# Loading the weights of dt on SyncE's queue ahead of the first tile of x, instead of on ScalarE's queue

## The chip, the cores and the metric

The kernel runs on one core of a Trainium2 chip. The metric is the device time of one execution in microseconds, lower is better. The profile of an execution covers a span that is a little shorter than that time: the span starts and ends with what the hardware profiler records on the engines.

Five engines work side by side, each through its own list of instructions in order: TensorE (PE, with PEld for its weight loads), VectorE (DVE), ScalarE (ACT), GpSimd (POOL) and SyncE (SP). Transfers between the chip's memory (HBM) and the on-chip SBUF are issued by an engine's instruction, and then run on 16 DMA engines. In this kernel nearly all loads are issued by SP; two of the first ones are issued by ACT.

## The reference

One layer of a hybrid decoder: 16 meta tokens are put ahead of 512 tokens, all 528 pass a norm, one large projection `w_in`, a pooling branch and a Mamba-2 branch, gates, an output projection and an MLP. What matters here is the start:

```
h = jnp.concatenate([meta, x], axis=1)
u = rmsnorm(h, mix_norm_w[i])
proj = u @ w_in[i]
xbc = proj[..., OFF_XBC:OFF_DT]
dt_raw = proj[..., OFF_DT:OFF_GATE]
...
dt = jax.nn.softplus(dt_raw + dt_bias)
```

`dt_raw` is a projection to only 32 columns, one for each head; `xbc` is one to 4096 columns.

## The kernel before

Features lie on the 128 partitions and tokens along the free axis, so x is eight tiles `xt[k]` of 128x528 (`NK` = 8, `L` = 528). Products run in a float32 form that TensorE takes in one pass with fewer bits, so every operand is split into a high part and a remainder: ACT casts to get the high part (`xh`, `whi`), DVE subtracts to get the rest (`xl`, `wlo`), and each product is three matmuls, high times high (line 141), high times rest (142) and rest times high (144). Line numbers are those of the profile.

**Weights** come as blocks of 128x1024 from `in_w`, in the order in which they are used. `block_tiles` hands out a buffer `raw` (three of them) and the split ones `whi` and `wlo` (four of each); `block_part` loads a block or a part of it on SP's queue (line 69), casts it on ACT (70) and subtracts on DVE (71). Block 0 holds the weights of dt: 256 columns, the 32 heads for each of the eight k. On the chip they are repeated four times (`once`, `spread`), so that the product has 128 rows. Block 1 holds the first block of B, its output tile is `px`.

**The start.** ACT issues `vs` (line 107: all vectors, the norm's scale among them) and then the 256 columns of dt's weights (line 178). SP issues x tile 0 (line 187), a quarter of block 1 (line 69), x tiles 1 and 2, the rest of block 1, x tiles 3 to 7, and then block after block. Meanwhile TensorE runs nine matmuls on a tile of ones (`WARM`, line 183), whose results nobody uses. Then:

- line 195: ACT casts the dt weights of k = 0 and 1; line 196: DVE subtracts
- line 190: ACT scales x tile k by the norm's weight, writes `xh`; line 191: DVE writes `xl`
- lines 200, 201: for k = 0 the products for dt (`pdt`, two runs of tokens) and for B (`px`)
- lines 203, 204: the dt weights of k = 2 to 7; line 206: the rest of block 1
- lines 209 to 225: the same for k = 2 to 7, with the squares of x for the norm (`square`, lines 211 to 215). The norm's factor is put on the results afterwards, so the products need not wait for it.

After the start the same pattern holds to the end: SP loads a block as soon as a `raw` buffer is free, ACT and DVE split it, TensorE multiplies.

**The order.** The text above is not quite the order in which an engine runs things. The framework's scheduler puts each engine's list together at build time, by priority (the order of the text) among what it expects to be ready, and adds the waits on semaphores. `ea` (line 279), for instance, stands far below the start in the text; it needs only `vs`, and it is ACT's first computation in the profile. Each engine then keeps its list strictly, waits included.

```
wdt, wB = block_tiles(), block_tiles()
b, raw, hi, lo = wdt
nc.scalar.dma_start(raw[:, :256], w[b, :, :256])
...
x_load(0)
act.copy(spread(hi)[:, :2], once[:, :2])
...
x_split(0)
block_part(wB, slice(0, 256))
```

Of the kernel before, what the change touches and what calls it, by code (L numbers as in the profile page):

```python
# [46 lines left out]
def kernel(ctx: ExitStack, tc, xT, x, w, vec, fnw, out):  # L47
    nc = tc.nc
# [126 lines left out]

    wdt, wB = block_tiles(), block_tiles()
    b, raw, hi, lo = wdt
    nc.scalar.dma_start(raw[:, :256], w[b, :, :256])
    spread = lambda t: t.rearrange("p (k c h) -> p k c h", c=4, h=HEADS)
    once = raw[:, :256].rearrange("p (k h) -> p k h", h=HEADS).unsqueeze(2).to_broadcast([P, NK, 4, HEADS])  # L180

# [872 lines left out]
```

## Time and profile before

| | |
|---|---|
| median of 3 runs | 1032.47 us (1031.5 to 1032.63) |
| the profiled execution, its own time | 1032.51 us |
| its span | 1030.8 us |
| PE busy | 1021.6 us of the span |
| DVE, ACT busy | 711.9, 541.3 us |
| moved by DMA | 105.62 MB, mean 102 GB/s |

How to read the views that follow: the timeline lists an engine's instructions in order, start, duration, engine, line, operation, what it writes and what it reads; in square brackets stands how long the engine was idle just before, and who released it. `ACTq` and `SPq` are the parts of ACT and SP that issue transfers. The chain of waits is followed back from the last instruction: at each step to what released it, or to the instruction before it on its engine. A transfer's "us to landing" counts from the issue to the moment when its semaphore says that all data is there. "PE" durations in the timeline are of single matmuls, which overlap; the chain shows their spacing.

### The profile page before, as it was taken

How to read it: one execution, taken by the hardware profiler on the slowest of the kernel's cores; microseconds unless marked ns; L12 is line 12 of the kernel's file. 1: busy time of each engine (PE TensorE's matmuls, PEld its weight loads, DVE VectorE, ACT ScalarE, POOL GpSimd, SP SyncE). 2: the span in 40 equal slices, each digit the busy share in tenths (PEclk: the TensorE clock that was granted, in tenths of full speed). 3: DMA queues.
4: the chain of work that ended last, by engine and by line, in shares of the span. 5: the costliest groups of instructions: out<-in, count | busy, mean ns of one | idle time of the engine just before them, and what ended most of it. 6: DMA issues, size and time to landing. Idle time of an engine off the chain costs nothing.

```text
span 1030.8 us, 14032 instructions
## 1 busy us (share of the span) xinstructions
PE 1021.6 (99%) x5721; PEld 883.2 (86%) x5721; DVE 711.9 (69%) x934; ACT 541.3 (53%) x706; POOL 9.9 (1%) x24
## 2 busy tenths in 40 slices
PE   9999999999999999999999999999999999999997
PEld 8889989998879898988998888888888888888886
DVE  7978787687646586878664345646686676776866
ACT  7775868586627339573443123345544355354444
POOL 0100000000000000000000000000000000000000
PEclk9999999999999999999999999999999999999999
DMA  6333051414332321413233323533323323333112
GB/s 232 95 139 102 22 164 31 154 46 139 102 107 79 104 102 41 146 54 114 78 105 99 102 82 102 204 127 132 89 83 122 109 80 120 101 102 123 42 41 82
DMA packets 29280, 105.62 MB, mean 102 GB/s; under 512 B 3296, under 2 KB 4256, under 8 KB 28192
## 3 DMA queue, kind: packets, MB, share of 16 engines
q1 hardware_dynamic: 26352, 92.61, 28.1%
q0 software_dynamic: 2000, 11.08, 2.9%
q8 instruction: 45, 0.74, 0.3%
q10 hardware_dynamic: 864, 1.04, 0.3%
q14 instruction: 19, 0.16, 0.0%
HBM read 102.55 MB, written 2.16 MB: 102 GB/s over the span
## 4 chain that ended last, share of the span: by engine, by line
PE 98%; DVE 1%; DMA 0%; ACT 0%; issue 0%; ACTq 0%
PE px L141 6%; PE px L142 6%; PE px L144 6%; PE pf L88 6%; PE pf L87 6%; PE pf L89 6%; PE alpha L797 3%; PE alpha L798 3%; PE alpha L799 3%; PE pz L141 3%; PE pz L142 3%; PE pz L144 3%; PE py L466 2%; PE pp L142 2%; PE pso L87 2%; PE pp L141 2%
## 5 line engine op out<-in xcount | busy, mean ns | idle before, releaser
L70 ACT CAST whi<-raw 128x1024 fp32r<-128x1024 f32 (+1 forms) x139 | 144.2, 1043 | 266.3 <-PE pf L88 59.9
L71 DVE TENSOR_TENSOR wlo<-raw,whi 128x1024 fp32r<-128x1024 f32 (+1 forms) x139 | 168.7, 1215 | 147.7 <-ACT whi L70 140.4
L141 PE MATMUL px<-uh,whi 128*128 128x264 f32 (+1 forms) x448 | 121.2, 290 | 0.7 <-DVE ct L330 0.7
L142 PE MATMUL px<-ul,whi 128*128 128x264 f32 (+1 forms) x448 | 118.9, 285 | 0.0
L88 PE MATMUL pf<-vl,whi 128*128 128x512 f32 x256 | 99.8, 390 | 0.0
L89 PE MATMUL pf<-vh,wlo 128*128 128x512 f32 x256 | 99.7, 389 | 0.0
L87 PE MATMUL pf<-vh,whi 128*128 128x512 f32 x256 | 99.6, 390 | 0.0
L144 PE MATMUL px<-uh,wlo 128*128 128x264 f32 (+1 forms) x448 | 90.8, 284 | 0.0
L141 PEld LDWEIGHTS px<-uh,whi 128*128 128x128 f32 x448 | 84.6, 189 | 2.8 <-issue 2.6
L142 PEld LDWEIGHTS px<-ul,whi 128*128 128x128 f32 x448 | 84.8, 189 | 0.3
L144 PEld LDWEIGHTS px<-uh,wlo 128*128 128x128 f32 x448 | 69.4, 188 | 0.3 <-issue 0.3
L748 DVE TENSOR_TENSOR slo<-b,shi 128x1024 fp32r<-128x1024 f32 x35 | 42.7, 1221 | 31.6 <-ACT shi L747 31.6
L747 ACT CAST shi<-b 128x1024 fp32r<-128x1024 f32 x35 | 36.7, 1050 | 51.9 <-PE pf L88 36.5
L88 PEld LDWEIGHTS pf<-vl,whi 128*128 128x128 f32 x256 | 48.0, 188 | 10.0 <-DVE vl L706 0.2
L87 PEld LDWEIGHTS pf<-vh,whi 128*128 128x128 f32 x256 | 48.1, 188 | 9.9
L89 PEld LDWEIGHTS pf<-vh,wlo 128*128 128x128 f32 x256 | 48.1, 188 | 9.9
L797 PE MATMUL alpha<-shi,hh 128*128 128x512 f32 x140 | 54.6, 390 | 0.0
L799 PE MATMUL alpha<-shi,hl 128*128 128x512 f32 x140 | 54.5, 389 | 0.0
L798 PE MATMUL alpha<-slo,hh 128*128 128x512 f32 x140 | 54.5, 389 | 0.0
L809 DVE TENSOR_TENSOR ht<-ht,alpha 128x1024 f32<-128x1024 f32 x35 | 42.6, 1217 | 6.1 <-PE alpha L799 6.1
L141 PE MATMUL pz<-uh,whi 128*128 128x512 f32 x112 | 44.0, 393 | 0.0
L142 PE MATMUL pz<-ul,whi 128*128 128x512 f32 x112 | 43.9, 392 | 0.0
(340 smaller groups left out, 2405.4 us busy)
## 6 DMA issues: line engine op xcount, KB each, us to landing
raw<-in_w SPq DMA_DIRECT2D x137, 512.0 KB, 3.6
b<-in_w SPq DMA_DIRECT2D x28, 512.0 KB, 3.6
abc<-acs_d POOLq DMA_DIRECT2D x8, 1024.0 KB, 7.5
xt<-in_xT SPq DMA_DIRECT2D x8, 264.0 KB, 5.2
ht<-in_x POOLq DMA_DIRECT2D x4, 512.0 KB, 4.9
w<-in_w SPq DMA_DIRECT2D x4, 512.0 KB, 3.5
out_dram<-out SPq DMA_DIRECT2D x4, 320.0 KB, 2.4
out_dram<-out ACTq DMA_DIRECT2D x4, 192.0 KB, 2.6
```

The costliest lines, as they stand in the source:

```text
L70: act.copy(hi[:, c], raw[:, c])
L71: dve.tensor_tensor(lo[:, c], raw[:, c], hi[:, c].bitcast(F32), op=ALU.subtract)
L87: pe.matmul(ps, ah, bh, start=first, stop=False)
L88: pe.matmul(ps, ah, bl, start=False, stop=False)
L89: pe.matmul(ps, al, bh, start=False, stop=last)
L141: pe.matmul(o, wh, rhs[0][k][:, c], start=k == 0, stop=False)
L142: pe.matmul(o, wh, rhs[1][k][:, c], start=False, stop=False)
L144: pe.matmul(o, wl, rhs[0][k][:, c], start=False, stop=k == NK - 1)
L748: dve.tensor_tensor(lo, src, hi.bitcast(F32), op=ALU.subtract)
L797: pe.matmul(ps[t], a[0], wh[:, cs], start=f, stop=False, skip_group_check=True)
L798: pe.matmul(ps[t], a[0], wl[:, cs], start=False, stop=False, skip_group_check=True)
L799: pe.matmul(ps[t], a[1], wh[:, cs], start=False, stop=l, skip_group_check=True)
```

## The change

The transfer of the dt weights is issued by SP instead of ACT. It stands ahead of `x_load(0)` in the text, so it becomes the first entry of SP's list, and x tile 0 becomes the second. ACT's queue keeps only `vs` at the start. Size, source, target and everything else in the text stay as they are.

```
     wdt, wB = block_tiles(), block_tiles()
     b, raw, hi, lo = wdt
-    nc.scalar.dma_start(raw[:, :256], w[b, :, :256])
+    nc.sync.dma_start(raw[:, :256], w[b, :, :256])
```

## The prediction

> **What bounds the kernel now.** I read the page's first part, the waits of TensorE, and then the first 13 us in the timeline and the chain of waits, since the change touches nothing later.
>
> ```profile
> span 1030.8 us, 14032 instructions
> PE 1021.6 (99%) x5721; PEld 883.2 (86%) x5721; DVE 711.9 (69%) x934; ACT 541.3 (53%) x706; POOL 9.9 (1%) x24
> ```
>
> ```profile
> PE pdt L183 <- DVE ones_r L97: 1.5, 1, 1.5
> PE pdt L141 <- ACT xh L190: 1.1, 1, 1.1
> PE px L141 <- DVE ct L330: 0.7, 1, 0.7
> ```
>
> TensorE is busy for 1021.6 of 1030.8 us. The three rows are all the waits of its matmuls: 1.5 us before the warming matmuls, 1.1 us between them and the first useful matmul, 0.7 us much later. So a head start of TensorE at the beginning goes through to the end, unless it then meets a wait that it does not have today. And nothing can be won from idle time but the second row's 1.1 us and the third's 0.7.
>
> The start, from the timeline (first three rows with the issues, then ACT, PE and DVE):
>
> ```profile
> 0.81 0.41 ACTq L107 DMA_DIRECT2D vs<-in_vec  x1
> 0.81 0.38 SPq L187 DMA_DIRECT2D xt<-in_xT  x1
> 1.25 0.42 SPq L69 DMA_DIRECT2D raw<-in_w  x1
> 1.25 0.45 ACTq L178 DMA_DIRECT2D raw<-in_w  x1
> 1.50 4.21 PE L183 MATMUL pdt<-ones_r 128*128 128x512 f32 x9 [1.50 <-DVE ones_r L97]
> 2.66 0.43 SPq L69 DMA_DIRECT2D raw<-in_w  x1
> 4.93 0.20 ACT L279 ACTIVATE ea<-vs 128x1 f32<-128x1 f32 x1 [1.93 <-DMA vs<-in_vec]
> 5.68 0.40 ACT L195 CAST whi<-raw 128x256 fp32r<-128x256 f32 x1 [0.54 <-DMA raw<-in_w]
> 5.99 0.73 ACT L190 ACTIVATE xh<-xt,vs 128x528 fp32r<-128x528 f32 x1
> 6.77 0.81 PE L141 MATMUL pdt<-xh,whi 128*128 128x272 f32 x2 [1.06 <-ACT xh L190]
> 8.45 0.83 ACT L70 CAST whi<-raw 128x768 fp32r<-128x768 f32 x1
> 10.19 0.22 DVE L102 COPY sel<-ident 128x128 f32<-128x128 f32 x1
> 10.46 1.45 DVE L191 SCALAR_TENSOR_TENSOR xl<-xt,vs,xh 128x528 fp32r<-128x528 f32 x2
> ```
>
> ACT does `ea` when `vs` is there (4.93), waits 0.54 us for the dt weights (5.68), casts them, and only then scales x tile 0 (5.99), which releases TensorE at 6.77. No wait stands before the row at 5.99: x tile 0 had landed, and it was the dt weights that held it up, through ACT's order. The warming matmuls end at 1.50 + 4.21 = 5.71; from there to 6.77 is the idle 1.06 us. The chain of waits says the same:
>
> ```profile
> 0.81 0.41 ACTq L107
> 1.22 0.03 issue
> 1.25 4.41 DMA raw<-in_w
> 5.66 0.02 issue
> 5.68 0.40 ACT whi L195
> 6.08 0.65 ACT xh L190
> ...
> 9.92 0.23 PE pdt L141
> 10.15 0.23 PE pdt L142
> 10.38 0.14 PE pdt L141
> 10.51 0.12 PE pdt L142
> ...
> 11.98 0.24 PE pdt L142 x2
> ```
>
> Its lower half shows one thing more: matmuls that follow each other by 0.23 us up to about 10.35, and by 0.12 us after it. TensorE runs at half pace for the first 3.6 us of its useful work.
>
> **The change, part by part.** It removes one issue from ACT (0.45 us at 1.25) and adds one to SP, at 0.81. SP issues one after the other, so everything behind it on SP is issued about 0.44 us later: x tile 0 at 1.25, the quarter of block 1 at about 1.70, and so on; nothing else moves on POOL or ACT. What counts is when each lands.
>
> ```profile
> xt<-in_xT SPq DMA_DIRECT2D x1, 264.0 KB, 3.9
> vs<-in_vec ACTq DMA_DIRECT2D x1, 117.0 KB, 4.1
> raw<-in_w SPq DMA_DIRECT2D x1, 128.0 KB, 4.2
> raw<-in_w ACTq DMA_DIRECT2D x1, 128.0 KB, 4.4
> raw<-in_w SPq DMA_DIRECT2D x1, 384.0 KB, 5.8
> ```
>
> ```profile
> 1.00:2.00 1.00, 0.49 (x1) 0.50 (x2) 0.42 (x3) 0.27 (x1) 0.54 (x3) 1.00 0.17 21
> 2.00:3.00 1.00, 1.00 (x4) 0.71 (x4) 0.00 (x0) 1.00 (x1) 0.00 (x0) 1.00 0.73 177
> 3.00:4.00 1.00, 1.00 (x4) 0.81 (x3) 0.00 (x0) 0.01 (x1) 0.00 (x0) 1.00 0.96 324
> 4.00:5.00 1.00, 1.00 (x4) 0.80 (x3) 0.00 (x0) 0.07 (x1) 0.00 (x0) 1.00 1.01 317
> ```
>
> The last two columns of the windows are the busy share of the 16 DMA engines and GB/s: from 3 us on the engines are full. So landings go by bytes ahead, not by the time of issue. Summed, 21 kB have moved at 2.0, 198 at 3.0, 522 at 4.0, 839 at 5.0. I assume that the two queues take turns row by row, each transfer having 128 rows. Then x tile 0 (270 kB) and `vs` (120) are through together at 390 kB, which is 3 + 192/324 = 3.59 us; they landed at 0.81 + 3.9 = 4.71 and 4.93, so 1.1 and 1.3 us after. The quarter of block 1 and the dt weights (131 each) are through at 652 kB, 4 + 130/317 = 4.41 us; they landed at 1.25 + 4.2 = 5.45 and 5.66, again 1.0 and 1.25 after. The assumption gives the same delay twice for each queue, so I use it for the new order.
>
> New order: dt weights and `vs` take turns and are through at 251 kB, 3 + 53/324 = 3.16 us; they land near 4.2 and 4.45. x tile 0 follows at 521 kB, 4.0 us, and lands near 5.1. The quarter of block 1 is at 652 kB as before and lands near 5.5. Bounds for x tile 0, the one price that the trace does not show: 0.81 + 3.9 = 4.71, where it lands now, from below; issued at 1.25 and as slow as the slowest load of these rows (5.8), 7.05 from above. I take 5.1, since 1.25 + 3.9 = 5.15 comes out beside it.
>
> ACT then: `ea` at 4.45 to 4.65, cast of the dt weights from about 4.65, x tile 0 after its landing at 5.1 instead of 5.99 (the cast leaves ACT free 0.31 us after its start, as from 5.68 to 5.99). TensorE follows 0.78 us after it, at 5.9 instead of 6.77. That is **0.87 us** of the 1.06, and it does not run into the warming matmuls (5.71). ACT's saved issue is worth nothing by itself: ACT then waits for `vs` anyway. Of the later loads only the rest of block 1 matters: it is issued at 3.1 instead of 2.66, behind the same bytes, and its cast starts at its landing (2.66 + 5.8 = 8.46 against the row at 8.45). I put that at no change; if the issue counted in full, it would cost 0.44 us there.
>
> What of the 0.87 arrives at the end? If the step to full pace stays at 10.35 us, the head start is 0.87 us of half pace, worth 0.87 x 0.12/0.23 = 0.45. If the step moves along with the start, it is worth up to 0.87, but then the next limit is x tile 2: its `xl` is written by 10.46 + about 0.76 (the row's two take 1.45) = 11.22, and its first use today is at 11.98, so at most 0.76 can be gained past it, because the cast at 8.45 that stands ahead of it on ACT waits for its transfer. So 0.45 to 0.76; I take **0.6 us**. After that no wait absorbs it except, perhaps, the 0.7 us behind line 330, which follows TensorE's own results and moves along.
>
> Sum: 1032.51 - 0.6 = **1031.9 us**, against the profiled execution's own time (span 1030.8 and 1.7 around it), which is 0.04 above the median of the three runs.
>
> [...]
>
> **The rivals.**
>
> *The clock comes earlier.* In the profile the 4.21 us of warming matmuls, followed by 1.06 us of nothing, left the useful matmuls at half pace until 10.35. With a hole of only 0.2 us the step could fall around 7. The half pace from 6.77 to 10.35 costs up to 3.58 x 0.48 = 1.7 us, and with the 0.87 about 2.5 could be had; x tile 2 caps it at 0.76 unless its work moves up too (the `sel` copies at 10.19 stand in front of it, 0.27 us to the next start). So 1.0 us, 1031.5 us, where the cap holds as in this profile, and up to 2.5, 1030.0 us, where today's step comes later than 10.35, so that x tile 2 isn't the next limit; I take 1030.2 for the case. Against it: the windows give a granted clock of 1.00 throughout, so they do not say what sets the step. [...]
>
> *Nothing arrives.* x tile 0 lands near 6.0, or `ea` and the cast are put in another order, and ACT starts it when it does today: 1032.5 us.
>
> *x tile 0 comes late.* Costs begin once it lands after 5.99. At 7.05, the upper bound, TensorE starts 1.06 us later: 1033.6 us; if the step to full pace slips in addition, by up to the 1.7 of above, 1035.3 us. For it: x tile 0 is issued second. Against it: it has fewer bytes ahead of it than the dt weights have now.
>
> *The order shifts: slower.* The rows at 4.93 and 10.19 show instructions of lines 279 and 102 far from their place in the text: the lists are made at build time from expected readiness, and the first landings change. If one weight block's split is then listed behind other work, TensorE meets it unfinished.
>
> ```profile
> L70 ACT CAST whi<-raw 128x1024 fp32r<-128x1024 f32 (+1 forms) x139 | 144.2, 1043 | 266.3 <-PE pf L88 59.9
> L71 DVE TENSOR_TENSOR wlo<-raw,whi 128x1024 fp32r<-128x1024 f32 (+1 forms) x139 | 168.7, 1215 | 147.7 <-ACT whi L70 140.4
> ```
>
> One block wholly late costs 1.04 + 1.22 = 2.3 us, so 1034.2 us with the gain counted; two cost 4.5 us, 1036.4 us, which I take as this case's time, since a list that has shifted at one block has reason to do it again. It decides from the point where a split is delayed by more than its lead over TensorE. Against it: ACT stands idle 266 us before these casts, most of it until TensorE frees a buffer, so leads are long.
>
> **How the numbers follow.** Chances: the forecast 0.46, the earlier clock 0.17, nothing arrives 0.10, late x 0.09, shifted order 0.18. A measurement of this kernel tells about 0.2% (2.1 us) from no change: faster needs 1030.4 or less, slower 1034.5 or more. Faster is two thirds of the clock's case (0.12), the rest of it staying under the cap. Slower is the order's case and most of the late x, with the step slipping too (0.18 + 0.07 = 0.25). The rest, 0.63, is within. The likeliest case alone spans 1031.5 to 1032.3. The range, 1030.0 to 1036.4, takes in the clock's best end, the late x and the shifted order up to two blocks.
>
> **What would show it.** Right: in the changed timeline the dt weights land first, `ea` and the cast of line 195 run by 5.1, line 190 starts with a wait on x tile 0 near 5.1, the first useful matmul stands near 5.9, and TensorE's waits are those of today with 1.06 become about 0.2. Wrong: a start of line 190 after 5.99 (the turns of the queues); a new TensorE wait behind `xl` of tile 2 beyond 0.1 us (the cap); spacing of 0.12 us before 9 us (the clock); any TensorE wait after 20 us that is not line 330's (the order).

## The result, and the profile after

| | before | changed |
|---|---|---|
| median of 21 runs each | 1032.13 us | 1030.79 us |
| lowest, highest | 1031.5, 1034.36 | 1030.47, 1031.26 |
| profiled execution: span | 1030.8 us | 1029.0 us |

The changed kernel takes 0.9987 of the time before (95% interval 0.9981 to 0.9993): 1.3 us less, faster but within the 0.2% that the prediction set as its bound. The forecast was 1031.9, a gain of 0.6 us. The span of the profiled execution shrank by 1.8 us, more than the median did; the reason comes below, and it is that the first profile of before was one of its slower executions.

The waits of TensorE's matmuls in the changed kernel, all of them (microseconds in total, times, longest):

```profile
PE pdt L183 <- DVE ones_r L97: 1.5, 1, 1.5
PE px L141 <- DVE ct L330: 0.7, 1, 0.7
PE pdt L141 <- ACT xh L190: 0.2, 1, 0.2
```

The 1.06 us ahead of the first useful matmul have become 0.2, and no wait has come in later in this execution (the second profile of the changed kernel, below, has two short ones). The start, from the timeline of the changed kernel:

```profile
0.80 0.38 SPq L178 DMA_DIRECT2D raw<-in_w  x1
1.24 0.42 SPq L187 DMA_DIRECT2D xt<-in_xT  x1
...
3.65 0.40 ACT L195 CAST whi<-raw 128x256 fp32r<-128x256 f32 x1 [1.12 <-DMA raw<-in_w]
4.67 0.74 ACT L190 ACTIVATE xh<-xt,vs 128x528 fp32r<-128x528 f32 x1 [0.61 <-DMA xt<-in_xT]
...
7.55 0.73 ACT L190 ACTIVATE xh<-xt,vs 128x528 fp32r<-128x528 f32 x1
8.18 0.82 ACT L70 CAST whi<-raw 128x768 fp32r<-128x768 f32 x1
...
8.56 0.76 DVE L191 SCALAR_TENSOR_TENSOR xl<-xt,vs,xh 128x528 fp32r<-128x528 f32 x1
...
1.50 3.74 PE L183 MATMUL pdt<-ones_r 128*128 128x512 f32 x9 [1.50 <-DVE ones_r L97]
5.46 0.51 PE L141 MATMUL pdt<-xh,whi 128*128 128x272 f32 x2 [0.22 <-ACT xh L190]
```

Three things are to be seen. **Line 190 starts 1.3 us earlier** (4.67 instead of 5.99), now released by x tile 0 itself, and TensorE follows at 5.46 instead of 6.77. **The warming matmuls take 3.74 us** instead of 4.21: from the second to the one at 4.22 they start 0.43 us apart, at the end 0.23 (4.61 and 4.84), so the last of them already run at full pace. In the profile before, it is 0.43 us from the second to the last. **x tile 2 is scaled before the rest of block 1 is cast** (7.55 before 8.18); in the profile before, the cast at 8.45 came first. Nothing in the diff says so. The chain of waits of the changed kernel confirms the pace from the first products on, 0.12 us a matmul:

```profile
1.24 3.34 DMA xt<-in_xT
...
4.67 0.75 ACT xh L190
5.41 0.03 issue
5.44 0.78 DVE xl L191
6.22 0.04 issue
6.26 0.52 PE pdt L142 x2
6.78 0.25 PE pdt L144 x2
7.03 0.12 PE px L142
7.15 0.12 PE px L141
```

The instruction lists of the two programs, put side by side, explain the third point. The first rows of ACT's list that differ:

```
-L279 LoadActFuncSet
-L279 Activation ea<-vs 128x1
+L195 LoadActFuncSet
 L195 TensorCopy whi<-raw 128x256
...
 L203 TensorCopy whi<-raw 128x768
+L190 Activation xh(2)<-xt(2),vs 128x528
 L70 TensorCopy whi<-raw 128x768
-L190 Activation xh(2)<-xt(2),vs 128x528
```

The number of the tile is put in brackets here. The scheduler found x tile 2 ready sooner and listed it first; `ea` moved behind the x tiles. On DVE `xl` of tile 2 moved ahead of the rest of block 1 in the same way. Taken from the two traces, the lists differ in places up to 48 us on TensorE, 60 on ACT and 64 on DVE, and hold the same computations in the same order after that. The time was won before any of the differences that lie beyond the start: the first product of x tile 4 stands at 14.37 us before and at 12.39 in the changed kernel, and from there to the end it takes 1016.4 and 1016.6 us.

So there are three candidates: **the start** (the transfers land earlier), **the clock** (full pace comes earlier), **the list** (x tile 2 ahead). The changed kernel has all three.

### The profile page after: what moved, and what is told of

Read it like the earlier page. It is cut to its first block, busy times and chain, and to the rows that moved or that the text cites. A ratio compares the mean times of both kernels' runs of the same rounds, so it can differ in the third digit from the quotient of the medians.

```text
span 1029.0 us, 14029 instructions
## 1 busy us (share of the span) xinstructions
PE 1020.4 (99%) x5721; PEld 882.0 (86%) x5721; DVE 711.9 (69%) x934; ACT 540.7 (53%) x706; POOL 9.9 (1%) x24
## 4 chain that ended last, share of the span: by engine, by line
PE 98%; DVE 1%; ACT 0%; DMA 0%; issue 0%; SPq 0%; ACTq 0%
PE px L141 6%; PE px L142 6%; PE px L144 6%; PE pf L87 6%; PE pf L89 6%; PE pf L88 6%; PE alpha L797 3%; PE alpha L799 3%; PE alpha L798 3%; PE pz L141 3%; PE pz L142 3%; PE pz L144 3%; PE py L466 2%; PE pp L142 2%; PE pso L87 2%; PE pp L141 2%
## 5 line engine op out<-in xcount | busy, mean ns | idle before, releaser
L141 PE MATMUL px<-uh,whi 128*128 128x264 f32 (+1 forms) x448 | 121.2, 290 | 0.7 <-DVE ct L330 0.7
L141 PEld LDWEIGHTS px<-uh,whi 128*128 128x128 f32 x448 | 84.6, 189 | 2.8 <-issue 2.6
L141 PE MATMUL pz<-uh,whi 128*128 128x512 f32 x112 | 44.0, 393 | 0.0
```

Of the source, the lines that this page charges most:

```text
L141: pe.matmul(o, wh, rhs[0][k][:, c], start=k == 0, stop=False)
```

## The experiments

All times are medians of 11 executions beside executions of the kernel before on the same chip, if nothing else is said. In the first four runs the kernel before took 1031.85 us, in the next three 1031.97, in the last three 1031.9. The interval of a ratio reaches about 0.9 us to either side, so most single ratios here do not exclude that nothing changed; what follows rests on the spread of the executions, on the profiles, and on medians of runs taken side by side.

**The transfer on SyncE's queue, but second.**

```
     x_load(0)
+    nc.sync.dma_start(raw[:, :256], w[b, :, :256])
     act.copy(spread(hi)[:, :2], once[:, :2])
```

> The dt weights go to SP's queue, but behind x tile 0 instead of ahead of it. Theory 'bytes' (landings go by the bytes ahead in both queues, and TensorE starts 0.78 us after line 190): vs (120 kB) and x tile 0 (270) are ahead of the dt weights (131), 521 kB in all, the same sum that x tile 0 has in the changed kernel, where it landed at 4.58. So the dt weights land near 4.6, line 190 starts near 4.9 to 5.0, the first useful matmul stands near 5.7, 0.25 later than in the changed kernel; time about 1.0 us under the kernel before. Rival 'first place' (the gain needs the dt weights ahead of x tile 0): start near 6.8, no gain. Theory 'clock' adds: warming ends near 5.2 to 5.7, the hole is under 0.5 us, so the useful matmuls run at 0.12 us spacing before 9 us.

Measured: 1031.04 us, ratio 0.9991 (0.9982 to 1.0), executions from 1030.77 to 1031.33. ACT in the timeline (L189 is the scaling of an x tile in this program):

```profile
4.64 0.41 ACT L195 CAST whi<-raw 128x256 fp32r<-128x256 f32 x1
4.95 0.73 ACT L189 ACTIVATE xh<-xt,vs 128x528 fp32r<-128x528 f32 x1
...
7.64 0.74 ACT L189 ACTIVATE xh<-xt,vs 128x528 fp32r<-128x528 f32 x1
8.29 0.82 ACT L70 CAST whi<-raw 128x768 fp32r<-128x768 f32 x1
```

The landing and the start (first useful matmul at 5.74) came out as "bytes" said, and "first place" is wrong: the dt weights need not stand ahead of x tile 0. (The warming matmuls end only at 5.71 here, so the start could not have been earlier in any case.) But this program has the new list, too, so it can't tell the start from the list.

**The dt weights first on ScalarE's queue.**

```
-    nc.scalar.dma_start(vs, vec)
...
     nc.scalar.dma_start(raw[:, :256], w[b, :, :256])
+    nc.scalar.dma_start(vs, vec)
```

> The dt weights stay on ACT's queue, but are issued there ahead of vs; x tile 0 stays first on SP. Theory 'bytes': dt weights and x tile 0 take turns from the start, vs comes last, all three through at 521 kB, so vs lands near 4.6 to 4.9, line 190 starts near 4.7 to 5.0, first useful matmul 5.5 to 5.8; a gain of 0.8 to 1.2 us without SP. Theory 'list' (part of the gain is that x tile 2 is scaled ahead of the cast of block 1's rest on ACT): here the list keeps the order of before, so TensorE waits for xl of tile 2 near 10.5 to 11, and the gain stays under 0.8 us. Rival 'SP' (the queue itself is what counts): time as before.

Measured: 1031.7 us, ratio 1.0 (0.9991 to 1.0009). Its waits of TensorE in the start (line numbers up to 177 are one lower in this program, so L141 is the product with `xl`):

```profile
...
PE pdt L141 <- DVE xl L191: 0.7, 1, 0.7
PE pdt L140 <- ACT xh L190: 0.6, 1, 0.6
```

Here `vs` landed later than "bytes" said (1.25 + 4.0 = 5.25), and TensorE started at 6.15. Full pace had come within the warming (4.01 us instead of 4.21). But x tile 2 stands behind the rest of block 1 as before, and the earlier start (0.6 us against the first profile of before) went into a new wait of 0.7 us for `xl` of tile 2, up to 11.05. That is the cap that the prediction had named, and it left 0.15 us at the median. The run above it, taken side by side and with x tile 2 ahead, is 0.66 us faster.

**The changed kernel with few warming matmuls.**

```
-WARM = 9
+WARM = 4
```

> The changed kernel with 4 instead of 9 warming matmuls. They end near 3.6, the useful ones start near 5.46 as before, after 1.9 us of nothing. Theory 'clock' (the continued work is what brings full pace early): spacing of 0.23 us up to about 9, k = 2 begins near 10.2 instead of 9.38, the time is 0.5 to 0.9 us above the changed kernel's. Rival 'data' (what lands and what is split sets the pace; the clock would have come anyway): first spacing of 0.12 us and a time within 0.2 us of the changed kernel's.

Measured: 1031.95 us, ratio 0.9998 (0.9989 to 1.0007). The executions fall in two groups: five from 1030.89 to 1031.47, six from 1031.95 to 1032.34. The profiled one (1032.24) is of the second; its timeline, and below it the chain of waits:

```profile
1.50 2.08 PE L183 MATMUL pdt<-ones_r 128*128 128x512 f32 x4 [1.50 <-DVE ones_r L97]
5.15 0.81 PE L141 MATMUL pdt<-xh,whi 128*128 128x272 f32 x2 [1.57 <-ACT xh L190]
```

```profile
11.17 0.23 PE pdt L142
11.39 0.14 PE pdt L141
11.53 0.12 PE pdt L142
```

The useful matmuls ran at half pace up to 11.4, later than expected. With the earliest start of all so far (5.15) this execution is as slow as the kernel before. The groups lie about 1.1 us apart. If the faster one holds the executions with early full pace, that is what a late clock costs, and it comes late only in some executions; of the faster group none was profiled.

**The kernel before, with x tile 2 ahead.** The load of the rest of block 1 stays where it was; only its cast and its subtract are written behind the split of x tile 2.

```
     x_load(2)
-    block_part(wB, slice(256, 1024))
+    rest = slice(256, 1024)
+    nc.sync.dma_start(wB[1][:, rest], w[wB[0], :, rest])
...
         x_split(k)
+        if k == 2:
+            act.copy(wB[2][:, rest], wB[1][:, rest])
+            dve.tensor_tensor(wB[3][:, rest], wB[1][:, rest], wB[2][:, rest].bitcast(F32), op=ALU.subtract)
```

> The kernel before with one thing of the changed kernel's list: x tile 2 is scaled on ACT ahead of the cast of the rest of block 1 (and its xl ahead of that block's subtract on DVE); all transfers as before. Theory 'start' (the gain comes from the earlier first matmul and the clock): first useful matmul at 6.8, and since TensorE had no wait at x tile 2 before, the time stays within 0.3 us of the kernel before. Rival 'list': a gain of 0.5 us or more.

Measured: 1031.23 us, ratio 0.9996 (0.9987 to 1.0005). Two groups again: seven executions from 1030.73 to 1031.46, four from 1032.26 to 1033.05. The profiled one (1030.92) has full pace (0.12 us a matmul from 7.45 on in its chain of waits) and starts at 6.13; all its waits of TensorE (L334 is line 330 of before):

```profile
PE pdt L183 <- DVE ones_r L97: 1.5, 1, 1.5
PE px L141 <- DVE ct L334: 0.7, 1, 0.7
PE pdt L141 <- ACT xh L190: 0.4, 1, 0.4
```

The median lies 0.62 us under the kernel before, as "list" said, but with two groups in it the ratio's interval includes no change. The expected start of 6.8 was wrong: the transfers of before landed earlier here than in the first profile. What the groups say is this: with the list alone, no transfer moved, seven of 11 executions run about as fast as the changed kernel. That the other four have the late clock is likely and not shown, since none of them was profiled.

**The kernel before, with more warming matmuls** (`WARM = 13`).

> The kernel before with 13 instead of 9 warming matmuls, so that no hole is left ahead of the first useful matmul; transfers and the order on ACT and DVE as before. Theory 'clock and list' (the changed kernel's gain is made of two things: full pace in every execution, and x tile 2 scaled ahead of the rest of block 1; the earlier landing matters only through them): full pace before 8 us in the profile, no execution above about 1032.2, but TensorE waits 0.5 to 0.8 us for xl of tile 2 near 11, as in the run with the dt weights first on ScalarE; median 1031.5 to 1031.8. Rival 'clock alone': median near the changed kernel's 1030.8. Rival 'start': median as before.

Measured: 1031.82 us, ratio 0.9999 (0.999 to 1.0008). No execution is above 1032.04, where the kernel before reached 1032.78 beside it: none lies where the late clock would put it. The median hardly moved (0.15 us), because the cap stays; the next run shows what it is worth. The chain of waits has it:

```profile
2.66 5.49 DMA raw<-in_w
8.14 0.02 issue
8.17 0.84 ACT whi L70
...
10.26 0.69 DVE xl L191
10.95 0.04 issue
10.99 0.51 PE pdt L142 x2
```

TensorE's first product with `xl` of tile 2 hangs on the transfer of the rest of block 1, through the cast that stands ahead of the tile on ACT. It waits about 0.3 us for it, less than the 0.5 to 0.8 expected, since the thirteen warming matmuls had put the first useful one at 7.21.

**Both at once on the kernel before** (the edit of x tile 2, and `WARM = 13`).

> Both at once on the kernel before: 13 warming matmuls, and x tile 2 ahead of the rest of block 1 on ACT and DVE. No transfer is moved. Theory 'clock and list': median within 0.3 us of the changed kernel's 1030.8, all executions between 1030.4 and 1031.5, none near 1032.5. Rival 'start' (the transfers' order itself is worth something): at least 0.5 us above the changed kernel, 1031.3 or more.

Measured: 1031.22 us, ratio 0.9994 (0.9985 to 1.0002), executions from 1030.96 to 1031.95. That is 0.4 above the changed kernel of the first measurement, more than "clock and list" allowed and just short of the rival; one execution (1031.95) is above the 1031.5 that was expected as the most. Against the run before it, taken side by side, the order of x tile 2 alone gains 0.60 us here, and against the kernel before the two together gain 0.75. TensorE has no listed wait between the warming and line 330's; in the chain of waits the warming matmuls go on past the data, which were there at 6.1:

```profile
4.86 2.48 PE pdt L183 x6
7.34 0.24 PE pdt L141 x2
```

The run with 11 below shortens that.

**The changed kernel with the old order.** The split of x tile 2 is queued behind the rest of block 1 on ACT and DVE; the transfers are those of the changed kernel.

```
-    block_part(wB, slice(256, 1024))
+    rest = block_part(wB, slice(256, 1024))
...
-        x_split(k)
+        if k == 2:
+            with tc.issue_after(rest[0].ins), tc.issue_after(rest[1].ins):
+                x_split(k)
+        else:
+            x_split(k)
```

Here `block_part` returns its cast and its subtract.

> The changed kernel's transfers, but x tile 2 queued behind the rest of block 1 on ACT and DVE, as before. Theory 'clock and list': TensorE waits 0.6 to 1.2 us for xl of tile 2, the median rises by 0.5 to 0.9 us to 1031.3 to 1031.7. Rival 'start': within 0.2 us of the changed kernel's 1030.8.

Measured: 1031.76 us, ratio 0.9999 (0.999 to 1.0008). Its waits of TensorE:

```profile
...
PE pdt L142 <- DVE xl L191: 0.8, 2, 0.4
PE px L141 <- DVE ct L334: 0.7, 1, 0.7
PE pdt L141 <- ACT xh L190: 0.2, 1, 0.2
```

This is the clearest of the runs. The change as written, with its early landing and no hole behind the warming, but with x tile 2 behind the rest of block 1, is level with the kernel before (0.2 us under it at the median, within the interval). The start is as early as in the changed kernel (5.51). Of the waits, the 0.4 us for `xl` of tile 1 is found in the second profile of the changed kernel as well; the new ones are 0.2 for `xh` and 0.4 for `xl` of tile 2, up to 10.97. The list is not quite the one of before: the square of line 211 came ahead of the cast of the rest of block 1 on ACT (7.87 before 8.42). By DVE's own row of work that delays `xl` of tile 2 by some 0.13 us, an estimate from this profile (the subtract of line 71 starts at 9.28 and could have started at 9.15), so most of the effect is the order's.

**The kernel before, profiled once more** (one execution).

> The kernel before, profiled once more, to see what differs between two executions of one program: theory 'clock' expects either the 0.23 us spacing up to 10 us again, or 0.12 us from about 7 us on and then a wait for xl of tile 2 near 11; and landings of the first transfers within 0.6 us of the first profile's.

Measured: 1031.71 us, span 1030.0. ACT and PE in its timeline:

```profile
5.59 0.73 ACT L190 ACTIVATE xh<-xt,vs 128x528 fp32r<-128x528 f32 x1
...
6.37 0.52 PE L141 MATMUL pdt<-xh,whi 128*128 128x272 f32 x2 [0.66 <-ACT xh L190]
...
10.87 0.51 PE L142 MATMUL pdt<-xl,whi 128*128 128x272 f32 x2 [0.52 <-DVE xl L191]
```

The second branch of the expectation: the same program as in the first profile, now at full pace (the first two products take 0.52 us instead of 0.81, and the starts from 7.76 on lie 0.12 us apart), and with the wait for `xl` of tile 2 that the half pace had hidden. The first profile's absence of that wait was no sign of slack.

**The changed kernel again, beside the last two.**

> The changed kernel again, on the same chip as the next two. Theory 'clock and list': full pace before 7 us, no execution above 1031.5, median near 1030.8, first transfers landing within 0.6 us of the first profile's.

Measured: 1030.9 us, ratio 0.999 (0.9981 to 0.9998), executions from 1030.67 to 1031.31. With the 21 of the first measurement, none of 32 executions is above 1031.31. The warming takes 3.87 us in its profile, against the 4.21 of half pace, so full pace came within it again. TensorE starts at 5.21, without a hole, and two short waits stand behind the start that the first profile of this kernel does not list, for the quarter of block 1 and for `xl` of tile 1:

```profile
PE px L141 <- ACT whi L70: 0.4, 1, 0.4
PE pdt L142 <- DVE xl L191: 0.4, 1, 0.4
```

So a start that is 0.25 us earlier than in the first profile gained nothing: the data behind it were not there.

**The kernel before with x tile 2 ahead and 11 warming matmuls.**

> The kernel before with x tile 2 ahead of the rest of block 1 on ACT and DVE, and 11 warming matmuls instead of 13 as in the earlier run, so that they end near 6.4 at full pace instead of 7.3, close to where the data come (6.1 to 6.8). No transfer is moved. This prices the earlier start by itself, with order and clock as in the changed kernel. Theory 'clock and list': 1030.8 to 1031.0, within 0.2 us of the changed kernel, since what TensorE gains by starting at 5.46 it loses again waiting for xl of tiles 0, 1 and 2. Rival 'start': 0.4 us or more above the changed kernel (the start is 0.7 to 1.3 us later at full pace).

Measured: 1031.14 us, ratio 0.9989 (0.998 to 0.9998), executions from 1030.72 to 1031.37. First useful matmul at 6.36, no later wait but line 330's, none of the executions late. The gain is 0.76 us of the changed kernel's 1.0, without any transfer moved. What is left for the earlier start is 0.24 us, between the two theories' numbers, and nearer to "clock and list"; drawing 11 executions again and again from those of each run puts it between 0.06 and 0.42 us in 95% of the draws. The price is not quite clean either: the warming still ends a little after the data (6.56), and the useful matmuls of this profile run at half pace until about 7.6 (0.57 us for the two of 7.05, 0.24 for the two of 7.62). Thirteen warming matmuls, with a start 0.8 us later, gained the same (0.75).

**The changed kernel with the `sel` copies late** (lines 102 and 103 queued on DVE behind the last `xl`).

> The changed kernel with the two sel copies on DVE (9.24 to 9.5 in its profile) queued behind the last xl, so that xl of tiles 3 to 7 come 0.27 us earlier. After tile 1 TensorE waits a little for each xl (0.27 us at tile 2, 0.2 at 3 and 4 between the matmuls' spacings). Theory 'list' (DVE's order sets the start once the clock is at full pace): 0.1 to 0.3 us under the changed kernel, 1030.5 to 1030.7. Rival: DVE is not what TensorE waits for after tile 2, and nothing changes.

Measured: 1031.04 us, ratio 0.999 (0.9981 to 0.9999), which can't be told from the 1030.9 of the changed kernel. The edit moved less than expected: the first product with `xl` of tile 3 starts at 11.15, against 11.22 and 11.44 in the two profiles of the changed kernel. So it brought nothing that the median shows, and no version in this study is faster than the changed kernel.

## Why the prediction was right, and where its steps were not

The direction was right, and the time lies in the range. That it does is partly luck: the range was wide for other reasons, and most of the gain came by a way that the forecast did not count on. The forecast gain of 0.6 us is less than half of the 1.3 measured. Where the kernel runs by the forecast's own mechanism, an earlier start with the cap in place, it takes 1031.76 (the changed kernel with the old order), near the 1031.9 that was forecast. Step by step it stands like this.

**The order of the bytes: right.** The dt weights and `vs` land first, x tile 0 after them, and the start of line 190 follows x tile 0. **The size of the landing: off by about half a microsecond.** The prediction had 4.2, 4.45 and 5.1; measured were 0.80 + 2.8 = 3.6 for the dt weights, 0.8 + 3.1 = 3.9 for `vs` and 4.58 for x tile 0. The term that was mis-sized is the 1.0 to 1.3 us between the last byte and the landing, taken from one profile; by the same reckoning with the windows of the changed profile it is 0.5 to 0.8. In six profiles with the transfers of before, the dt weights took 3.8 to 4.4 us from issue to landing and x tile 0 took 3.1 to 3.9, and the first profile has the largest number of both:

```profile
xt<-in_xT SPq DMA_DIRECT2D x1, 264.0 KB, 3.1
...
raw<-in_w ACTq DMA_DIRECT2D x1, 128.0 KB, 3.9
```

These two rows, from the issues by transfer with KB and us to landing, are of the run with 11 warming matmuls. So the start moved to 5.46 instead of 5.9. `ea` did not run before the cast, as the prediction had it, but at 15.26, behind the x tiles.

**What of it arrives: the step that failed.** The prediction carried the head start to the end, up to a cap of 0.76 us past x tile 2 "because the cast at 8.45 that stands ahead of it on ACT waits for its transfer". The cap was real. In the changed kernel with the old order and in the run with ScalarE's queue it took nearly the whole head start (1031.76 and 1031.7 against 1031.9 or so before). What was wrong was to take ACT's order as fixed. The prediction knew that lists are made from expected readiness, and priced that only as a rival to the slow side; that the work of x tile 2 might move up stands in it as a mere "unless". The scheduler listed x tile 2 ahead, the cap was gone, and that makes most of the gain. Across two batches whose kernels before differ by 0.07 us it is 1031.76 - 1030.9 = 0.86 us; side by side, with no transfer moved, it is 0.60 (13 warming matmuls without and with x tile 2 ahead). The earlier start by itself is worth 0.24 us or so (the run with 11 warming matmuls against the changed kernel).

The profiles of all runs say the same. Counted are the first useful product and the first product of x tile 3, which is the first one past the cap:

| x tile 2 and the rest of block 1; pace | profiles | first useful product | first product of x tile 3 | span |
|---|---|---|---|---|
| x tile 2 behind; full pace by 7.6 us | 4 | 5.51 to 7.21 | 12.08 to 12.24 | 1030.0 to 1030.1 |
| x tile 2 ahead; full pace by 7.8 us | 7 | 5.21 to 7.18 | 10.85 to 11.53 | 1029.0 to 1029.6 |
| half pace past 10 us: first profile of before, few warming matmuls | 2 | 6.77, 5.15 | 12.90, 12.46 | 1030.8, 1030.5 |

With x tile 2 behind, x tile 3 comes at the same time whether TensorE starts at 5.5 or at 7.2. With x tile 2 ahead it comes 0.6 to 1.4 us earlier, and the start again matters less than the order.

**The clock: the rival came true as well.** The prediction gave a chance of 0.17 to a step of the clock near 7; the 7 was a guess of the author's that no row of the profile gives. The step fell at 4.5 in the changed kernel's profile, already within the warming, so the sign that the prediction had named for it (0.12 us before 9 us) was there. This is worth nothing in the executions of before that had full pace early, and up to 1.1 us in the others (the groups of the run with four warming matmuls). It would explain why the changed kernel's executions lie within 0.8 us (21 runs) while before has ten of 21 above 1032.3. It does explain why the two first profiles differ by 1.8 us and the medians by 1.3: the first profile of before was an execution with the late clock, and the second one, with full pace, is only 0.8 us of span above the changed kernel's second. The prediction held that the windows do not say what sets the step, as they show a granted clock of 1.00. The trace's own record of the clock shows where the step falls (10.28 and 4.54 us in the two first profiles), but what sets it no run shows, as the last section has it.

**No new wait after 20 us: right.** TensorE's waits in the first changed profile are those of before with 1.06 become 0.2; the two of the second stand before 9 us. "Nothing arrives" and "x tile 0 comes late" did not happen. "The order shifts" did, to the other side.

**SyncE's busier list: no loss seen.** The 0.44 us that later loads are issued later show up nowhere as a loss: the rest of block 1 was issued at 3.15 and landed at 7.85, against 8.46 in the first profile of before and by 7.88 in the second, where its cast starts without a wait.

What stays open: the three parts do not add up like terms of a sum, since each hides the others (full pace without the list is worth 0.15 us at the median, and the list alone left four executions of 11 slow). How much the clock alone gives the changed kernel at the median was not separated from the 0.2 to 0.3 us of the start. And that the slower groups are executions with the late clock is shown for the two that were profiled, and argued for the rest.

## What to carry to other kernels

Where a scheduler makes the lists, a change to one transfer is also a change to the order of everything that became ready at another time; look for the instruction that stands ahead of the next limit, and ask whether it may be passed. A wait that a profile does not show may be hidden behind a slower engine, so a second profile of the same program is worth having before slack is read from the first: here the 0.5 us for `xl` of tile 2 stand in the second profile of before alone. TensorE's pace changed early in this kernel (from 0.23 to 0.12 us a matmul), and work without a hole ahead of the real data went with a steadier time, though not in every run: in the seven runs whose profile has no hole behind the warming the executions of a run lie within 0.4 to 1.6 us, in the five with a hole of 0.2 us or more within 0.8 to 2.9. How far it may reach past the data's arrival is not settled here: an end at 6.56 and one at 7.34 gained the same.

## What the runs showed of the hardware

**One landing, several durations.** The same two transfers with the same queues ahead of them took 3.1 to 3.9 and 3.8 to 4.4 us from issue to landing in six profiles. A delay taken from one execution is good to some half microsecond.

**When full pace comes.** The granted clock stands at 1.00 in the rows of the windows from 0 us on, while the matmuls' spacing goes from 0.23 to 0.12 us at one point. In the two first profiles the trace's own record of the granted clock begins with a stretch at full clock just where the spacing changes: at 10.28 us in that of before and at 4.54 in that of the changed kernel. With four warming matmuls the spacing changes at 11.39 us. In the ten other profiles it is 0.12 to 0.13 us, waits apart, from 7.8 us on at the latest.

The two late ones are those with the longest holes behind the warming, 1.06 us (the first profile of before) and 1.57 (four warming matmuls); in the other eleven the hole is at most 0.66 us. That the hole is what makes the step late is an estimate from these 13 profiles. What sets the point is not shown: without a hole it came within the warming, so before 5.4 us, in the second profile of the changed kernel, at about 7.6 in the run with 11 warming matmuls, and at 7.6 to 7.8 in the run with the transfer second. And one program differs from one execution to the next: the second profile of before, with a hole of 0.66 us, was at full pace where the first one, with 1.06, was not.
